# The mixer's output projection as seven products of halves, with memory's keys and values moved in front of it

## The chip, the cores and the metric

The kernel runs on one core of one Trainium2 chip. The metric is the device time of one execution in microseconds; the page of the profile and the trace come from one profiled execution. TensorE (PE) multiplies, VectorE (DVE) and ScalarE (ACT) work on tiles in on-chip memory, GpSimd (POOL) does a little elementwise work and issues the accumulating DMAs, SyncE (SP) issues most loads.

## The reference

One decoder layer for 512 tokens of width 2048 in float32: a mixer of three groups (12 heads of dilated attention, 8 heads of forgetting attention, 4 heads of gated linear attention, GLA) with one output projection, cross-attention of 4 heads into 256 memory tokens, and a gated MLP of width 5504; each has an RMSNorm in front and a residual add behind.

```python
mixed = jnp.concatenate([o_a, o_b, o_c], axis=-1)          # 512 x 2048
x = x + mixed @ w_out                                       # 2048 x 2048
mem_n = rms_norm(mem, mem_norm)
q = rms_norm(x, norm_cross) @ w_q
k, v = jnp.split(mem_n @ w_kv, 2, axis=-1)
...
x = x + memory_cross_attention(...)
x = x + conv_ffn(rms_norm(x, norm_ffn), w_up, conv_w, conv_b, w_down)
return rms_norm(x, norm_final)
```

## The kernel before

**Precision and form.** Activations lie transposed, 128 features on the partitions and 512 tokens along the row, in 16 tiles. Each operand of a large product is split into a high part (ScalarE's copy into float32r) and a low part (VectorE's subtraction); a product takes three matmuls: hi-hi, hi-lo, lo-hi (`mm3`, L367 to 373). Weights come as raw blocks of 128 x 1024 (512 KB), five buffers (`wraw`), and are split in halves of 512 columns into five buffers each of `whi` and `wlo` (`weights` L337 to 360, `split_weights` L326 to 332).

**Order.** Instructions are put in each engine's queue by a scheduler at build time, which goes by the order of the program and by what it reckons to be ready; each engine then works through its queue in that order. `issue_after(ins)` holds an instruction behind another one of the same engine. Work of the attention heads is written as generators; `tick` advances them by `rate` steps while the projections' units run (`run`, `W_A`, `W_B`, `W_O`, ...), so that the heads' small matmuls lie among the large ones. The score and transpose matmuls are put behind the last large one (`behind`).

**Mixer.** After the first projections and the GLA (`gla`, which ends with a power on POOL at L839), the pairs of heads of groups A and B are projected (`qk_units`) and attended (`attend`). Their 16 results, tiles of 128 x 512 in `self.mix`, lie in the pools `mc` and `mab` (`stream`, L266 to 269). The output projection then takes them as 16 pairs of split tiles (`mtile`, `split`, L314 to 319) and multiplies 16 x 16 blocks with 512 columns each: 32 weight blocks `w_o` of 512 KB, two for each of the 16 output tiles. The first halves of four output tiles run while the last heads finish (`W_O`). Each output tile is added to x from a raw load (`resid`, `raw_tile`) and squared for the next norm (`square`: even tiles are summed on POOL, odd ones on VectorE).

**Memory and cross-attention.** During the later output tiles, `memory` loads and splits the memory tokens and sums their squares. `cross` then runs memory's keys and values (8 blocks of `w_ck` with 256 columns, 8 blocks of `w_cv`) and, among them, the 16 splits of the residual for the queries (`more`) and the norm's root (`rms`, at unit `ST`). The query products, their heads and the output projection `w_co` follow.

**Sums of weights.** The MLP's up projection already works by seven products of halves: for blocks a11, a12, a21, a22 of the operand and b11 to b22 of the weights, seven products of sums of blocks take the place of eight (`product`, L1359 and following, `UP_ORDER`). Sums of weights for some tiles are made in DRAM by accumulating DMAs from POOL (`added`, L1258 to 1272, each behind the one before by `self.turn`): `first_sums` (11 transfers, held behind the last POOL square of the residual, `self.pooled`) and `up_sums` (8). They are issued at the beginning of the query products. During the cross output projection, `squares` (L1197 to 1204) makes ScalarE squares in three buffers `xsqt`, and POOL adds them by accumulating DMAs; `token_sums` (L1318 and following) makes the operands of the up projection.

## Time and profile before

| | us |
|---|---|
| median of 3 runs (lowest, highest) | 2306.24 (2304.97, 2306.7) |
| profiled execution | 2308.35 |
| its span, first to last instruction | 2306.2 |
| TensorE busy in the span | 2282.7 |
| VectorE, ScalarE, POOL busy | 1845.7, 1242.3, 204.9 |
| mean granted TensorE clock | 0.998 |

The span is what the trace covers; the profiled execution takes 2.15 us more. A matmul's record runs to its modelled end, which overlaps the next one's start, so the distance between starts is what a matmul costs. Rows of groups give the line, engine, operation, output and inputs by name, shapes, count, busy time and mean in ns. In a table of stretches the counts stand in brackets.

### The profile page before, as it was taken

What the parts mean: (1) busy time and instruction counts of PE and PEld (TensorE: products, weight loads), DVE (VectorE), ACT (ScalarE), POOL (GpSimd) and SP (SyncE); (2) the same over time, 40 slices, a digit from 0 to 9 for tenths busy, and PEclk for the clock granted to TensorE, in tenths of its full rate; (3) what the DMA queues carried; (4) which work ended last, traced back from release to release, by engine and by line L of the source; (5) the groups of instructions that cost most, each with busy time, mean ns of one, the idle gap of its engine ahead of it and who ended that gap; (6) DMA issues with size and microseconds to landing.
All of it is one profiled execution on the core that took longest, in us unless ns stands there. A gap on an engine that the chain in (4) does not pass through costs nothing.

```text
span 2306.2 us, 42646 instructions
## 1 busy us (share of the span) xinstructions
PE 2282.7 (99%) x15948; PEld 2140.1 (93%) x15948; DVE 1845.7 (80%) x3620; ACT 1242.3 (54%) x2545; POOL 204.9 (9%) x278
## 2 busy tenths in 40 slices
PE   9999999999999999999999999999999999999997
PEld 8798898888778888899999999999999999999997
DVE  7825666666797355699999999999999898999887
ACT  6323345655575254585555555555555575747454
POOL 3000000000002011121111111100000020101003
PEclk9999999999999999999999999999999999999999
DMA  6432122223224358587777778753334493736432
GB/s 217 152 97 83 49 98 91 93 87 96 87 80 153 110 180 218 132 233 180 214 209 213 205 209 215 199 184 122 130 126 140 142 337 103 277 115 230 154 122 84
DMA packets 130836, 355.47 MB, mean 154 GB/s; under 512 B 13653, under 2 KB 45333, under 8 KB 130181
## 3 DMA queue, kind: packets, MB, share of 16 engines
q1 hardware_dynamic: 87264, 268.28, 34.5%
q0 software_dynamic: 37168, 73.91, 14.6%
q10 hardware_dynamic: 6196, 10.57, 1.4%
q8 instruction: 125, 2.05, 0.4%
q14 instruction: 83, 0.67, 0.1%
HBM read 325.65 MB, written 76.07 MB: 174 GB/s over the span
## 4 chain that ended last, share of the span: by engine, by line
PE 91%; DVE 4%; DMA 2%; ACT 2%; issue 1%; POOL 0%; DVEq 0%; SPq 0%; ACTq 0%
PE acc L369 18%; PE acc L371 18%; PE acc L370 18%; PE psC L371 5%; PE psC L369 5%; PE psC L370 5%; PE psD L370 3%; PE psD L369 3%; PE psD L371 3%; PE acc L410 2%; PE acc L411 2%; PE acc L412 2%; PE psS L783 1%; PE psT L551 1%; PE psQ L371 1%; PE psQ L370 1%
## 5 line engine op out<-in xcount | busy, mean ns | idle before, releaser
L330 ACT ACTIVATE whi<-wraw 128x512 fp32r<-128x512 f32 (+2 forms) x814 | 466.1, 602 | 431.7 <-DVE wraw L1384 177.2
L331 DVE TENSOR_TENSOR wlo<-wraw,whi 128x512 fp32r<-128x512 f32 (+2 forms) x814 | 517.1, 655 | 83.5 <-ACT whi L330 78.8
L371 PE MATMUL acc<-sum,wlo 128*128 128x256 f32 x1956 | 549.3, 281 | 0.9 <-DVE wlo L331 0.8
L370 PE MATMUL acc<-sum,whi 128*128 128x256 f32 x1956 | 549.7, 281 | 0.0
L369 PE MATMUL acc<-sum,whi 128*128 128x256 f32 x1956 | 548.4, 280 | 0.0
L356 DVE TENSOR_TENSOR wlo<-wraw,whi 128x512 fp32r<-128x512 f32 (+2 forms) x336 | 223.0, 671 | 200.3 <-ACT whi L355 199.2
L355 ACT ACTIVATE whi<-wraw 128x512 fp32r<-128x512 f32 (+2 forms) x336 | 203.3, 610 | 325.1 <-PE acc L370 210.1
L371 PEld LDWEIGHTS acc<-sum,wlo 128*128 128x128 f32 x1956 | 368.5, 188 | 1.7 <-DVE wlo L331 1.7
L369 PEld LDWEIGHTS acc<-sum,whi 128*128 128x128 f32 x1956 | 368.5, 188 | 0.6 <-ACT whi L330 0.4
L370 PEld LDWEIGHTS acc<-sum,whi 128*128 128x128 f32 x1956 | 367.9, 188 | 0.0
L369 PE MATMUL acc<-xhi,whi 128*128 128x512 f32 (+1 forms) x848 | 334.8, 395 | 0.4 <-ACT fg L890 0.4
L371 PE MATMUL acc<-xhi,wlo 128*128 128x512 f32 (+1 forms) x848 | 329.1, 388 | 0.0
L370 PE MATMUL acc<-xlo,whi 128*128 128x512 f32 (+1 forms) x848 | 328.5, 388 | 0.0
L371 PE MATMUL psC<-sum,wlo 128*128 128x256 f32 x928 | 261.1, 281 | 0.0
L369 PE MATMUL psC<-sum,whi 128*128 128x256 f32 x928 | 260.3, 280 | 0.0
L370 PE MATMUL psC<-sum,whi 128*128 128x256 f32 x928 | 259.7, 280 | 0.0
L371 PEld LDWEIGHTS acc<-xhi,wlo 128*128 128x128 f32 x848 | 159.4, 188 | 32.0
L369 PEld LDWEIGHTS acc<-xhi,whi 128*128 128x128 f32 x848 | 159.6, 188 | 29.1 <-ACT fg L890 0.8
L370 PEld LDWEIGHTS acc<-xlo,whi 128*128 128x128 f32 x848 | 159.8, 188 | 28.5 <-DVE xlo L318 0.2
L369 PEld LDWEIGHTS psC<-sum,whi 128*128 128x128 f32 x928 | 175.0, 189 | 0.0
L370 PEld LDWEIGHTS psC<-sum,whi 128*128 128x128 f32 x928 | 174.7, 188 | 0.0
L371 PEld LDWEIGHTS psC<-sum,wlo 128*128 128x128 f32 x928 | 174.5, 188 | 0.0
(401 smaller groups left out, 4359.3 us busy)
## 6 DMA issues: line engine op xcount, KB each, us to landing
wraw<-in_w_up SPq DMA_DIRECT2D x127, 512.0 KB, 6.2
b<-in_w_up SPq DMA_DIRECT2D x42, 512.0 KB, 4.5
wraw<-in_w_o SPq DMA_DIRECT2D x32, 512.0 KB, 3.5
wraw<-in_w_d SPq DMA_DIRECT2D x34, 448.0 KB, 4.4
wraw<-in_w_d SPq DMA_DIRECT2D x36, 384.0 KB, 4.6
wraw<-in_w_qka SPq DMA_DIRECT2D x24, 512.0 KB, 3.5
gd<-sq SPq DMA_DIRECT2D x40, 256.0 KB, 6.2
wraw<-two SPq DMA_DIRECT2D x20, 512.0 KB, 5.5
```

What stands on the lines that cost most here:

```text
L330: nc.scalar.activation(hi, r, AF.Copy)
L331: nc.vector.tensor_tensor(lo, r, hi.bitcast(F32), op=ALU.subtract)
L355: nc.scalar.activation(hi, r, AF.Copy)
L356: nc.vector.tensor_tensor(lo, r, hi.bitcast(F32), op=ALU.subtract)
L369: nc.tensor.matmul(out, lh, rh, start=start, stop=False, skip_group_check=more)
L370: nc.tensor.matmul(out, lh, rl, start=False, stop=False, skip_group_check=more)
L371: last = nc.tensor.matmul(out, ll, rh, start=False, stop=stop, skip_group_check=more)
L410: self.nc.tensor.matmul(o, xh[:, tt], wh, start=(k == 0), stop=False)
L411: self.nc.tensor.matmul(o, xh[:, tt], wl, start=False, stop=False)
L412: self.last = self.nc.tensor.matmul(o, xl[:, tt], wh, start=False, stop=(k == KT - 1))
L551: nc.tensor.transpose(tp[:, b * P:(b + 1) * P], pt[:, b * P:(b + 1) * P], self.ident)
L783: nc.tensor.matmul(sc[:, c * 64:(c + 1) * 64], kk[:, c * P:(c + 1) * P], qe[:, c * 64:(c + 1) * 64], start=True, stop=True)
```

## The change

- The 16 mixed tiles now lie in eight pairs (`mixed`, `stream`), in an order (`MIX_PAIRED`) that puts the blocks for the halves side by side.
- `out_sums`, right behind the GLA, issues for each of eight units the four sums of weight blocks in DRAM: eight transfers of 512 KB by `added`, 64 in all, on POOL. The first waits for the GLA's power, which is now `self.turn`; what was held behind the old `turn` is held behind `forgot`.
- `keys_values` takes the place of `memory` and of the first part of `cross`. It runs right behind the last B projection, with the last heads among its units (`W_M`): memory is loaded, split and squared in freed activation slots (`xlo`, `xhi`); keys and values are kept as float32 (`mkey`, `mval`) and split later (`halved`, in the first query product).
- `project` makes the seven operands of each of four groups (`operands`, the function that the up projection uses too) and runs eight units of seven products, 24 matmuls of 256 columns each, for two output tiles of 128 x 512 at a time. x is loaded into the tiles of the residual, and each product's result is added or subtracted there. In the last unit the products have another order (`OUT_ORDER`), and the splits for the queries are made there, in tiles that the products leave (`more`).
- In `cross` the norm's root and `halved` stand behind the first unit of the first query head.

```diff
+OUT_ORDER = (4, 5, 1, 6, 7, 3, 2)
...
+MIX_PAIRED = [MIX_ORDER[4 * v + 2 * e + i] for v in range(4) for i in range(2) for e in range(2)]
...
-        nc.gpsimd.tensor_tensor(ssf, ssf, self.mhalf, op=ALU.pow)
+        self.turn = nc.gpsimd.tensor_tensor(ssf, ssf, self.mhalf, op=ALU.pow)
...
-            self.turn = nc.scalar.activation(self.fg[:, t, :], ps[:, 384:G0], AF.Copy, scale=self.rs[:, t:t + 1])
+            self.forgot = nc.scalar.activation(self.fg[:, t, :], ps[:, 384:G0], AF.Copy, scale=self.rs[:, t:t + 1])
...
         es_core.close()
         es_gl.close()
+        self.out_sums()
...
-        units = [self.out_units(d["w_o"], n, Lazy(), evac_o(n)) for n in range(KT)]
-        self.rate = W_O / 2
-        for n in range(4):
-            units[n][0]()
-            self.tick()
-        self.rate = 0
+        self.keys_values()
         self.flush()
         es_ab.close()
         es_vv.close()
...
-        for n in range(4):
-            units[n][1]()
-        mem = self.memory()
-        for n in range(4, KT):
-            for u in units[n]:
-                u()
-                if n >= M0:
-                    next(mem, None)
+        self.project()
+
+    def keys_values(self):
+        nc, d = self.nc, self.d
+        raws = [self.xtile("xlo") for _ in range(8)]
+        mem = []
+        for j, raw in enumerate(raws):
+            two = raw.rearrange("p (i c) -> p i c", c=MEM)
+            nc.sync.dma_start(out=two, in_=d["memT"][j // 2][:, j % 2 * 2:j % 2 * 2 + 2, :])
+            for i in range(2):
+                t = self.xtile("xhi", F32R)
+                mem.append(self.split_to(t[:, :MEM], t[:, MEM:], two[:, i, :], self.gain(4, 2 * j + i)))
+            nc.scalar.activation(raw, raw, AF.Square)
+            if j > 1:
+                nc.vector.tensor_tensor(raws[j % 2], raws[j % 2], raw, op=ALU.add)
...
+        units = self.nat_units(d["w_cv"], 0, lambda k: mem[k], MT, evac_v)
+        units.insert(6, stats)
+        units += [u for h in range(X_HEADS) for u in self.out_units(d["w_ck"], h, mem, evac_k(h), MEM)]
+        self.run(units, W_M)
+
+    def out_sums(self):
+        self.o_pre = []
+        for n in range(KT // 2):
+            b11, b12, b22, b21 = [self.d["w_o"][4 * n + i] for i in range(4)]
+            t = [self.dr.tile([P, 1024], F32, name="o%d%d" % (n, i)) for i in range(4)]
+            self.added(t, b11, b12, b22, b21)
+            self.o_pre.append(t)
+
+    def operands(self, v, y, s, place):
...
+        src = {1: a11, 2: a12, 4: a22, 5: sa, 6: sb, 3: sb, 7: sa}
+        made = {5: (a22, a21, ALU.subtract), 6: (sa, a11, ALU.add), 3: (sb, a12, ALU.subtract),
+                7: (a21, a11, ALU.subtract)}
+        def part(j):
+            if j in made:
+                nc.vector.tensor_tensor(src[j], made[j][0], made[j][1], op=made[j][2])
+            th, tl = [place[j, v, n].rearrange("p (i c) -> p i c", c=HT) for n in range(2)]
+            split = nc.scalar.activation(th, src[j], AF.Copy)
...
+            nc.vector.tensor_tensor(tl, src[j], th.bitcast(F32), op=ALU.subtract)
+        return part
+
+    def project(self):
...
+        pa, pb = self.pool(self.es_a, "oa", "right"), self.pool(es_b, "ob", "right")
...
+        for v in range(NV - 1):
+            for j in (1, 5, 2, 6, 3):
+                parts[v](j)
...
+        def unit(n):
+            x = self.stream(n)
+            nc.sync.dma_start(out=x, in_=d["xT"][n])
+            w = [d["w_o"][4 * n + i] for i in range(4)]
+            pre = self.o_pre[n]
+            src = {1: w[0], 5: pre[0], 2: w[3], 6: pre[1], 3: w[2], 4: pre[2], 7: pre[3]}
...
+            for j in OUT_ORDER if last else UP_ORDER:
+                if n == 0:
+                    for v in range(NV) if j in (4, 7) else (NV - 1,):
+                        parts[v](j)
+                ps = bank[j][:, :HT]
+                self.product(j, self.halves(self.up_raw(src[j])), ps, j in (1, 5, 6, 4), True)
+                after(j, ps)
+                if last and j == 5:
+                    more(8, 4, 5)
+                if last and j == 7:
+                    more(6, 7, 1)
+            self.x1 += [x[:, 0, :], x[:, 1, :]]
+            for dt in (2 * n, 2 * n + 1):
+                self.square(dt, self.x1[dt], sqs, lambda c: tmps[dt % 2])
+            if last:
+                more(2, 7, 1)
...
+        def halved():
+            for a, th, tl in [(self.mkey[h], kh[h], kl[h]) for h in range(X_HEADS)] + list(zip(self.mval, vh, vl)):
+                nc.scalar.activation(th, a, AF.Copy)
+                nc.vector.tensor_tensor(tl, a, th.bitcast(F32), op=ALU.subtract)
+
+        def root():
+            box["R"] = self.rms(self.sqs, S, self.con.tile([P, S], F32, name="R", tag="R"))
...
         for h in range(X_HEADS - 1):
-            self.run(self.out_units(d["w_cq"], h, hs, evac_q(h, 0, NT)), W_X)
+            units = self.out_units(d["w_cq"], h, hs, evac_q(h, 0, NT))
+            if h == 0:
+                units.insert(1, root)
+                units.insert(2, halved)
+            self.run(units, W_X)
```

In `after(j, ps)`, two results are copied by ScalarE (`s1`, `s5`), and nine additions or subtractions of 128 x 256 on VectorE put the seven products together in the tiles of x.

More of the change, by code (lines that the diff above doesn't have):

```diff
@@ L72 @@
 W_B = 4
-W_O = 6
+W_M = 3
 W_X = 8
 WARM = 8
-M0 = 8
-H0 = 4
-H1 = 6
-ST = 4
 E0 = 14
@@ L264, in pool, with stream, mixed @@
         return es.enter_context(self.tc.tile_pool(name=name, bufs=1, side=side, reuse_waits="tile"))
-    def stream(self, k):
-        pool = self.mc if k < 6 else self.mab
-        return pool.tile([P, S], F32, name="str", tag="str", bufs=6 if k < 6 else 10)
+    def stream(self, n):
+        pool = self.mc if n < 3 else self.mab
+        return pool.tile([P, 2, S], F32, name="str", tag="str", bufs=3 if n < 3 else 5)
+    def mixed(self, m):
+        n = MIX_ORDER.index(m)
+        if n // 2 not in self.pairs:
+            self.pairs[n // 2] = self.stream(n // 2)
+        self.mix[m] = self.pairs[n // 2][:, n % 2, :]
+        return self.mix[m]
     def advance(self, n):
@@ L309, in xslot, with xtile @@
     def xslot(self, n=S):
-        hi = self.xp.tile([P, n], F32R, name="xhi", tag="xhi", bufs=KT, padded_shape=[P, S])
-        lo = self.xp.tile([P, n], F32R, name="xlo", tag="xlo", bufs=KT, padded_shape=[P, S])
-        return hi, lo
+        return self.xtile("xhi", F32R, n), self.xtile("xlo", F32R, n)
+    def xtile(self, tag, dtype=F32, n=S):
+        return self.xp.tile([P, n], dtype, name=tag, tag=tag, bufs=KT, padded_shape=[P, S])
     def split(self, src, n=S):
@@ L1327, in token_sums @@
             y.append(t)
[L1328 to L1344 removed]
+        sums = [tmp.tile([P, 2, HT], F32, name=n, tag=n, bufs=1) for n in ("sa", "sb")]
+        return self.operands(v, y, sums, place)
     def up_raw(self, u, pool=None):
```

199 lines of the change are left out of this document (94 added, 105 removed).

## The prediction

> **What bounds the kernel now.** I read the page's first lines, then a table by stretches (length, then busy time of PE, PEld, DVE, ACT and POOL with instruction counts, granted clock, DMA share, GB/s), then the order of the instructions where it matters.
>
> ```profile
> span 2306.2 us, 42646 instructions
> PE 2282.7 (99%) x15948; PEld 2140.1 (93%) x15948; DVE 1845.7 (80%) x3620; ACT 1242.3 (54%) x2545; POOL 204.9 (9%) x278
> ```
>
> ```profile
> 600.00:649.00 49.00, 47.49 (x236) 39.28 (x235) 36.53 (x100) 30.28 (x68) 0.00 (x0) 1.00 0.27 89
> 649.00:661.50 12.50, 12.50 (x62) 10.41 (x61) 12.49 (x38) 12.28 (x30) 0.00 (x0) 1.00 0.17 50
> 661.50:706.50 45.00, 43.81 (x219) 34.93 (x218) 39.17 (x115) 28.49 (x69) 0.00 (x0) 1.00 0.26 92
> 706.50:853.00 146.50, 146.50 (x656) 121.55 (x656) 72.63 (x113) 60.77 (x113) 23.49 (x24) 1.00 0.43 142
> 853.00:898.00 45.00, 45.00 (x288) 41.07 (x287) 31.53 (x53) 26.83 (x45) 4.10 (x4) 1.00 0.95 248
> 898.00:966.00 68.00, 67.69 (x377) 56.12 (x376) 40.27 (x99) 30.52 (x78) 8.20 (x10) 1.00 0.66 157
> 966.00:1015.00 49.00, 48.95 (x258) 42.11 (x257) 46.82 (x77) 45.89 (x84) 11.30 (x14) 1.00 0.71 170
> 1400.00:1700.00 300.00, 300.00 (x2546) 300.00 (x2545) 279.87 (x439) 160.68 (x287) 16.47 (x21) 1.00 0.56 168
> ```
>
> TensorE has work almost everywhere at full clock, so the kernel is as long as its matmuls plus the places where something else comes late. 661.5 is the end of the last B projection. From there to 706.5 the last attention heads run among the first matmuls of the output projection and VectorE is near its limit (39.17 of 45). From 706.5 to 853 TensorE alone binds; then memory's keys and values, 45 us. In 966 to 1015 (cross output projection, operands of the up projection) ScalarE (45.89 of 49) and VectorE (46.82) bind.
>
> **The matmuls.** What counts is the distance of their starts. The start time and duration of two hi-hi matmuls of the output projection, 13 groups of three apart, then the first copy of each up tile:
>
> ```profile
> 708.62 0.40 PE L369 MATMUL acc<-xhi,whi 128*128 128x512 f32 x1
> ...
> 717.48 0.39 PE L369 MATMUL acc<-xhi,whi 128*128 128x512 f32 x1
> ```
>
> ```profile
> L1414 ACT ACTIVATE s<-acc x42: 363/384/385, 1029.4 to 1843.3; 128x256 f32<-128x256 f32 x42
> ```
>
> 8.86 us by 39 is 0.227 us for 512 columns. An up tile is seven products of 24 matmuls of 256 columns: (1843.3 - 1029.4) / 41 = 19.85 us, 0.118 each. The projection has 16 x 16 x 3 = 768 of the wide ones, 174.5 us. After the change it is eight such units, 1344 narrow ones, 158.8 us. **Saved: 15.7 us.**
>
> The Trainium skill ("TensorE: Matmul & The Clock Gate", section "Back-to-back issue gap") gives 131 ns for 512 columns and 81 ns for 128; by a straight line between, 256 would cost 0.75 of 512, not half. The trace does not agree: 227 and 118 ns, 0.52.
>
> **What VectorE gets before and in the first unit.** Counts in 661.5 to 706.5, and three operand subtractions in a row on the chain (start, duration):
>
> ```profile
> L356 DVE TENSOR_TENSOR wlo<-wraw,whi 128x512 fp32r<-128x512 f32 x10 | 6.8, 687 | 0.7 <-PE psS L539 0.5
> L318 DVE TENSOR_TENSOR xlo<-str,xhi 128x512 fp32r<-128x512 f32 x7 | 4.7, 680 | 0.7 <-ACT xhi L317 0.7
> ```
>
> ```profile
> L318 DVE TENSOR_TENSOR xlo<-str,xhi x16: 669/680/693, 650.0 to 706.4; 128x512 fp32r<-128x512 f32 x16
> ```
>
> ```profile
> L371 PE MATMUL acc<-xhi,wlo 128*128 128x512 f32 x43 | 17.0, 395 | 0.0
> ```
>
> ```profile
> 975.24 1.81 DVE sum L1342 x3
> ```
>
> ```profile
> L574 DVE TENSOR_TENSOR str<-psO,ot x20: 682/689/695, 388.2 to 705.0; 64x512 f32<-64x512 f32 x20
> ```
>
> ```profile
> L323 DVE SCALAR_TENSOR_TENSOR xlo<-str,gains,xhi 128x512 fp32r<-128x512 f32 x6 | 4.4, 742 | 0.0
> L1063 DVE TENSOR_TENSOR kf<-acc,R 128x256 f32<-128x256 f32 x4 | 1.7, 420 | 0.3
> ```
>
> So 0.60 us for each 128x512 in a row (0.68 alone), 0.66 with a gain (0.74 alone), and about 0.35 for 128x256 (0.42 alone); the last two are estimates, less the same 0.07. From 661.5 to the last product of unit 0 VectorE then has:
> - the heads: 39.17 less 17 x 0.60 = 28.9;
> - keys and values: 32 weight splits (19.4), 16 memory splits of 256 columns (5.6), 6 square sums (3.6), less the 6.6 that it can do in the place of nine activation splits and two more before 661.5: 22.0; four key results 1.4;
> - operands of the seven products, all four groups: 28 low parts and 16 sums or differences, 44 x 0.60 = 26.6. The 16 low parts that they replace fell into 650 to 706. They cannot start earlier: their tiles lie where the attention's and values' tiles lie until the last head's result at 705 (L574), or in activation slots in use until 661;
> - unit 0: 14 weight splits 8.5, six results 2.1.
>
> Sum 89.5. TensorE has there: 45 less 129 projection matmuls (3 x 43) x 0.227 = 15.7 for the heads with their gaps; keys and values with the memory statistics 46; unit 0 19.85: 81.5. VectorE is 8 over at full use, 13 at the 95% that it reaches in 966 to 1015. **Added: 11 us**, bounds 5 and 17. Units 1 to 6 give VectorE 14 splits, 9 results and a square sum, 12.3 of 19.85, and hide all of it. ScalarE is nowhere over: it gains some 7 us of operand parts.
>
> **The last unit and what follows.** The first query matmul, behind the last of memory's values:
>
> ```profile
> 897.68 0.39 PE L412 MATMUL acc<-whi,mlo 128*128 128x512 f32 x1
> 897.91 0.39 PE L369 MATMUL acc<-xhi,whi 128*128 128x512 f32 x1
> ```
>
> The 16 splits of the residual for these queries lay beside memory's products (853 to 898, VectorE 31.5 of 45). Now they lie in the last unit: 12.3 + 16 x 0.66 = 22.9 on VectorE against 19.85, and behind it come the two norm splits, three norm steps and eight splits of keys and values, 7 us, in the first query product. That is some 3 us more than fits; the later splits have some time. **Added: 2.5 us**, bounds 0 and 6. So the query products would start 15.7 - 11 - 2.5 = **2 us earlier** than at 897.91.
>
> **The weight sums.** 64 transfers, eight for each unit, on POOL's queue, behind the GLA's power at 318:
>
> ```profile
> 318.04 2.91 POOL L839 TENSOR_TENSOR oss<-oss,mhalf 128x16 f32<-128x16 f32 x1 [31.62 <-DVE oss L838]
> 843.50 1.35 POOL L1046 TENSOR_TENSOR sq<-sq,sqt 128x512 f32<-128x512 f32 x1 [20.97 <-ACT sqt L1044]
> 844.79 2.10 POOL L1308 DMA_DIRECT2D pre<-in_w_up  x4
> 849.69 1.09 POOL L1312 DMA_DIRECT2D pre<-in_w_up  x1 [2.81 <-DMA pre<-in_w_up]
> ...
> 908.54 0.90 POOL L1262 DMA_DIRECT2D up<-in_w_up  x1
> ...
> 948.49 1.01 POOL L1262 DMA_DIRECT2D up<-in_w_up  x1 [6.60 <-DMA up<-in_w_up]
> 971.32 0.90 POOL L1204 DMA_DIRECT2D sq<-xsqt  x1 [21.81 <-ACT xsqt L1203]
> ```
>
> ```profile
> up<-in_w_up POOLq DMA_DIRECT2D x12, 512.0 KB, 7.4
> up<-up POOLq DMA_DIRECT2D x4, 512.0 KB, 3.9
> ```
>
> One set of eight takes 40 us from first issue to last (908.54 to 948.49), so some 42 with the next issue. With the lighter traffic before 660 (DMA share 0.27 against 0.66), 42 to 48: done at 321 + 8 x 44 = 673, bounds 657 and 705. Unit 0 starts near 725: hidden. The sums' traffic falls beside the attention's weight loads; 1400 to 1700 carries loads and such sums at DMA 0.56 with TensorE full: nothing, bounds 0 and 5. A unit then loads seven blocks of 512 KB in 19.85 us, 185 GB/s, about what that stretch moved (168): nothing. Its x load waits on SP until a pair of mixed tiles is free (in unit 0: until an operand 4 or 7 of the first group), with weight loads queued behind; five weight buffers, 14 us of products, cover it: nothing, bounds 0 and 3. POOL's power for memory's statistics stands behind the 64 sums; it is wanted near 695 (661.5, 21.8 for 96 value matmuls at 0.227 and 12 of the heads' 15.7): nothing either, but that is the thinnest cover here.
>
> **The next sums on that queue** are the up projection's, and they carry the price. They wait for the residual's last POOL square. It ended at 844.8, 53 us ahead of the query products, under memory's products; now it ends some 3 us behind their start. From that square to the issue of the last sum went 948.5 - 844.8 = 103.7 us. Part of it was traffic (853 to 898 at DMA 0.95). Without: copies 4.9, seven sums at about 6 us (40), the set of eight 40: 85; bounds 80 and 103.7. POOL is then free at 88 us behind the start of the query products, but the first square of the cross residual wants it at 971.3 - 897.9 = 73.4. It comes 15 us late.
>
> ```profile
> L1203 ACT ACTIVATE xsqt<-str x14: 614/618/633, 970.4 to 1011.3; 128x512 f32<-128x512 f32 x14
> L1204 POOL DMA_DIRECT2D sq<-xsqt x14: 862/864/899, 971.3 to 1015.0; - x14
> ...
> DMA to landing us min/median/max: 3.3/5.4/7.9
> ```
>
> ```profile
> 981.38 0.62 ACT L1203 ACTIVATE xsqt<-str 128x512 f32<-128x512 f32 x1
> ```
>
> The squares have three buffers. The fourth, at 981.38, needs the first one's transfer, 971.3 + 5.4: slack 4.7. So ScalarE would stand some 10 us in its queue, in the stretch where it is busy 45.89 of 49, with the weight splits of the cross output and the up operands behind the waiting square, then VectorE, then TensorE behind those. **Added: 10 us**, bounds 0 (in time) and 25 (103.7 + 3 - 73.4 - 4.7 = 29, less what an earlier start takes off). I take 10 as the 0.66 stretch is nearest to the new traffic.
>
> The Trainium skill ("TensorE: Matmul & The Clock Gate", section on the 16 sub-arrays) calls the GpSimd queue strict first in, first out; the POOL rows above, sums before squares, agree. Its page "DMA: Bandwidth & Descriptors", section "Anatomy of one DMA — SWDGE (gpsimd) path", puts such a transfer at 2.0 us plus bytes / 436e3, 3.2 us for 512 KB. The trace has 3.9 for a copy and 7.4 for a sum; by the page the first rival below would hold.
>
> **Sum.** -15.7 + 11 + 2.5 + 10 = **+8 us**. The profiled execution took 2308.35 us, 2.15 around its span; the runs' median is 2306.24, so I put the change on the median: **2314 us**, its own range 2308 to 2330.
>
> **Rivals.**
> 1. *The sums are out of the way.* If the 19 transfers take copies' time, 19 x 3.9 = 74, or the squares are issued between them, no square waits: -15.7 + 11 + 2.5 = -2, **2304** (2299 to 2309). For it: 21.81 us of spare time before. Against it: 7.4 for a sum.
> 2. *Faster: VectorE does not bind either.* It sat idle 12 us in 600 to 649; if parts of the operands and the first splits fall there, or are spread into unit 1, only the matmuls count: -15.7 + 2.5 = **2293** (2288 to 2299). Against it: the tiles' places.
> 3. *Slower: POOL's 64 sums run late.* At 50 us a set they end at 721, 20 to 25 us behind the wish of memory's statistics; ScalarE's copy of memory's values waits, and with it every later weight split: 2314 + 20 = **2334**. It decides from 47 us a set.
> 4. *The narrow matmul at 0.75 of the wide one* in this kernel's new place: 1344 x 0.170 = 228.9, +54: **2360**. Against it: the up units have them at 0.118. The first page's straight line would give this.
>
> **Chances.** Forecast 0.37, first rival 0.28, second 0.24, third 0.08, fourth 0.03. Within 0.2% is 2301.6 to 2310.9, about what a measurement can tell. Faster: all of the second and 0.08 of the first, 0.32. Same: 0.18 of the first and 0.05 of the forecast, 0.23. Slower 0.45. The range 2291 to 2330 leaves out the lower edge of the second, most of the third and the fourth.
>
> **What would show it.** Right: unit 0 near 30 us with TensorE waiting for VectorE's operand parts, units 1 to 6 at 19.85; POOL's first square issue of the cross residual well behind its ScalarE square, and ScalarE idle for that transfer. Wrong: units slower than 19.85; ScalarE waiting for a POOL power near 700; the query products more than 8 us from 896; the squares issued as soon as they are made.

## The result, and the profile after

| | median, us | runs | profiled span, us | clock |
|---|---|---|---|---|
| before | 2305.60 | 4 (2304.47 to 2306.70) | 2306.2 | 0.998 |
| after | 2339.64 | 4 (2338.79 to 2340.83) | 2337.0 | 0.991 |

The changed kernel takes 1.0148 times as long, 95% interval 1.013 to 1.0166: 34 us slower. The direction was as forecast, the size was not (+8). The first lines of the page of after:

```profile
span 2337.0 us, 44230 instructions
PE 2280.4 (98%) x16532; PEld 2161.0 (92%) x16532; DVE 1912.7 (82%) x3751; ACT 1280.1 (55%) x2617; POOL 248.7 (11%) x333
```

TensorE is busy 2.3 us less than before, although the narrow matmuls should have taken 15.7 off it, and it is idle some 33 us more. To find the place I compared two marks that both kernels have: the first scaled query (`cqf`, behind the first query product), and the first copy of an up tile. The rows are from the view of one tile; they give minimum, median and maximum duration in ns, then the first and the last start. First before, then after:

```profile
L1157 DVE SCALAR_TENSOR_TENSOR cqf<-acc,R x5: 423/690/692, 909.0 to 957.9; 128x512 f32<-128x512 f32 x3, 128x256 f32<-128x256 f32 x2
```

```profile
L1231 DVE SCALAR_TENSOR_TENSOR cqf<-acc,R x5: 425/692/693, 923.0 to 972.0; 128x512 f32<-128x512 f32 x3, 128x256 f32<-128x256 f32 x2
L1478 ACT ACTIVATE s<-acc x42: 361/386/389, 1061.2 to 1873.9; 128x256 f32<-128x256 f32 x42
```

The first query is 14.0 us late (909.0 to 923.0). From there to the first up tile it takes 138.2 us against 120.4 (1029.4 in the prediction less 909.0): 17.8 us more. Behind that the two run alike within 1.2 us. Up to the last B projection, near 661, both kernels run alike. So there are two losses, 31.8 us together. (The two profiled executions, 2308.35 and 2338.79, lie 30.4 us apart, the medians 34.0.)

**The first loss, 661 to 772.** The table by stretches of after (columns as in the prediction):

```profile
660.00:665.00 5.00, 4.37 (x21) 3.14 (x19) 5.00 (x16) 5.00 (x15) 0.00 (x0) 1.00 0.69 172
665.00:670.00 5.00, 1.86 (x8) 0.90 (x7) 5.00 (x15) 5.00 (x14) 0.00 (x0) 0.89 0.00 0
670.00:675.00 5.00, 0.00 (x0) 0.00 (x0) 4.77 (x16) 4.15 (x9) 0.00 (x0) 0.50 0.21 48
675.00:680.00 5.00, 4.35 (x15) 3.49 (x15) 4.76 (x9) 1.45 (x4) 0.00 (x0) 0.59 0.50 125
...
735.00:770.00 35.00, 29.88 (x224) 27.36 (x223) 32.59 (x58) 19.60 (x36) 0.00 (x0) 1.00 0.69 224
770.00:890.00 120.00, 120.00 (x1010) 119.89 (x1009) 88.80 (x149) 64.82 (x112) 10.30 (x8) 1.00 0.64 194
890.00:895.00 5.00, 2.75 (x17) 2.14 (x17) 5.00 (x9) 3.81 (x8) 0.00 (x0) 0.91 0.00 0
```

Where TensorE stands, VectorE is full: 660 to 680 (19.53 of 20, and ScalarE 10.00 of 10 in the first half) and 735 to 770. Between them it has gaps:

```profile
661.50:722.00 60.50, 51.27 (x287) 42.22 (x288) 52.62 (x149) 42.73 (x102) 0.82 (x1) 0.92 0.41 122
722.00:772.00 50.00, 44.88 (x349) 42.25 (x348) 47.50 (x85) 33.56 (x62) 0.27 (x1) 1.00 0.63 201
```

The waits of 655 to 690 (engine, tile and line that waited, what ended it: us in total, times, longest):

```profile
PE acc L420 <- DVE wlo L365: 7.3, 1, 7.3
...
ACT xhi L331 <- DMA xlo<-in_memT: 3.7, 1, 3.7
```

The memory loads are issued from 649.0 on, as the last B projection's matmuls leave the slots that they go to, and the first has landed at 655.4; all 16 memory splits and 8 squares then lie on ScalarE and VectorE, among the heads' own work, ahead of the value weights' splits, and TensorE waits 7.3 us for one of these. That delays the heads too. The last head's result and the first low part of an operand, in order of time (start, duration), and the first residual tile done, on POOL:

```profile
722.25 0.69 DVE L583 TENSOR_TENSOR str<-psO,ot 64x512 f32<-64x512 f32 x1
722.98 1.29 DVE L1026 TENSOR_TENSOR osum<-str,osum 128x512 fp32r<-128x512 f32 x2
```

```profile
771.73 2.54 POOL L1132 TENSOR_TENSOR sq<-str 128x512 f32<-128x512 f32 x2 [69.08 <-DVE str L1059]
786.10 1.29 POOL L1138 TENSOR_TENSOR sq<-sq,xlo 128x512 f32<-128x512 f32 x1 [11.82 <-ACT xlo L1136]
806.07 1.30 POOL L1138 TENSOR_TENSOR sq<-sq,xlo 128x512 f32<-128x512 f32 x1 [18.68 <-ACT xlo L1136]
...
886.20 1.30 POOL L1138 TENSOR_TENSOR sq<-sq,xlo 128x512 f32<-128x512 f32 x1 [18.92 <-ACT xlo L1136]
911.46 2.26 POOL L1138 TENSOR_TENSOR sq<-sq,xlo 128x512 f32<-128x512 f32 x1 [23.97 <-ACT xlo L1136]
913.67 2.04 POOL L1387 DMA_DIRECT2D pre<-in_w_up  x4
...
1006.34 1.01 POOL L1341 DMA_DIRECT2D up<-in_w_up  x1 [9.28 <-DMA up<-in_w_up]
1006.99 2.19 POOL L1283 DMA_DIRECT2D sq<-xsqt  x2
```

The operands start at 723 (the prediction took 705) and unit 0 is done at 771.7. From unit 1 to unit 6 the units come at 19.97 to 20.2 us (806.07 - 786.10 is the first), near the forecast's 19.85; the last takes 25.3 (911.46 - 886.20).

Unit 1 is done only 14.4 us behind unit 0. While unit 0's last product (`acc<-xhi`) waits for its parts, TensorE puts matmuls of unit 1's first products (`acc<-osum`, `psC<-xlo`) between:

```profile
769.09 0.28 PE L378 MATMUL acc<-osum,whi 128*128 128x256 f32 x1
769.45 0.38 PE L379 MATMUL acc<-xhi,whi 128*128 128x256 f32 x1
```

Some 50 of unit 1's 168 are done when unit 0 ends, 6 us of work at 0.119 each. So unit 0's mark overstates what was lost, and unit 1's is the safer one.

**The second loss, 1006 to 1030.** The same rows show POOL's queue: the up projection's sums from 913.67 to 1006.34, and only then the residual's squares. The waits of 980 to 1030:

```profile
ACT xsqt L1282 <- DMA sq<-xsqt: 18.7, 1, 18.7
DVE wlo L365 <- ACT whi L364: 18.3, 1, 18.3
...
PE acc L378 <- ACT sum L1023: 16.1, 1, 16.1
```

ScalarE waits 18.7 us for a buffer of squares, VectorE for the weight split behind it, TensorE for the operand behind that.

### The profile page after: what moved, and what is told of

Read it like the earlier page. It is cut to its first block, busy times and chain, and to the rows that moved or that the text cites. A ratio compares the mean times of both kernels' runs of the same rounds, so it can differ in the third digit from the quotient of the medians.

```text
span 2337.0 us, 44230 instructions
## 1 busy us (share of the span) xinstructions
PE 2280.4 (98%) x16532; PEld 2161.0 (92%) x16532; DVE 1912.7 (82%) x3751; ACT 1280.1 (55%) x2617; POOL 248.7 (11%) x333
## 3 DMA queue, kind: packets, MB, share of 16 engines
q0 software_dynamic: 55088, 107.47, 21.6%
## 4 chain that ended last, share of the span: by engine, by line
PE 55%; issue 2%; DVE 2%; DMA 2%; ACT 1%; POOL 1%; DVEq 0%; ACTq 0%; POOLq 0%
PE acc L380 10%; PE acc L379 10%; PE acc L378 10%; PE psC L380 5%; PE psC L378 5%; PE psC L379 5%; PE psD L379 3%; PE psD L380 3%; PE psD L378 3%; PE psQ L380 1%; PE psQ L379 1%; PE psQ L378 1%; DMA up<-in_w_up 1%; DMA pre<-in_w_up 1%; DVE sum L1026 0%
## 5 line engine op out<-in xcount | busy, mean ns | idle before, releaser
L339 ACT ACTIVATE whi<-wraw 128x512 fp32r<-128x512 f32 (+2 forms) x926 | 536.0, 606 | 500.2 <-DVE wraw L1448 176.5
L340 DVE TENSOR_TENSOR wlo<-wraw,whi 128x512 fp32r<-128x512 f32 (+2 forms) x926 | 596.2, 663 | 108.5 <-ACT whi L339 101.1
L365 DVE TENSOR_TENSOR wlo<-wraw,whi 128x512 fp32r<-128x512 f32 (+2 forms) x272 | 179.5, 668 | 155.3 <-ACT whi L364 154.9
L364 ACT ACTIVATE whi<-wraw 128x512 fp32r<-128x512 f32 (+2 forms) x272 | 162.4, 605 | 235.5 <-PE acc L379 123.8
L378 PE MATMUL acc<-xhi,whi 128*128 128x512 f32 (+1 forms) x720 | 271.0, 376 | 1.2 <-ACT whi L364 0.6
L380 PE MATMUL acc<-xhi,wlo 128*128 128x512 f32 (+1 forms) x720 | 265.7, 369 | 0.0
L379 PE MATMUL acc<-xlo,whi 128*128 128x512 f32 (+1 forms) x552 | 214.5, 389 | 0.0
L379 PEld LDWEIGHTS psC<-sum,whi 128*128 128x128 f32 x928 | 174.5, 188 | 0.0
L380 PEld LDWEIGHTS acc<-xhi,wlo 128*128 128x128 f32 x720 | 135.7, 188 | 22.9 <-DVE wlo L365 0.4
L378 PEld LDWEIGHTS acc<-xhi,whi 128*128 128x128 f32 x720 | 135.9, 189 | 21.2 <-ACT whi L364 0.9
L420 PE MATMUL acc<-wlo,xhi 128*128 128x384 f32 (+2 forms) x352 | 125.9, 358 | 8.2 <-DVE wlo L365 8.2
```

What stands on the lines that cost most here:

```text
L339: nc.scalar.activation(hi, r, AF.Copy)
L340: nc.vector.tensor_tensor(lo, r, hi.bitcast(F32), op=ALU.subtract)
L364: nc.scalar.activation(hi, r, AF.Copy)
L365: nc.vector.tensor_tensor(lo, r, hi.bitcast(F32), op=ALU.subtract)
L378: nc.tensor.matmul(out, lh, rh, start=start, stop=False, skip_group_check=more)
L379: nc.tensor.matmul(out, lh, rl, start=False, stop=False, skip_group_check=more)
```

## The experiments

All are edits of the changed kernel. Ratios are against the kernel before, run on the same chip; the changed kernel itself has 1.0148. "Unit 0 done" is POOL's first square of the residual, "query" and "up" are the two marks. The marks are of one execution each: e1_sums changes nothing ahead of 771, and its last head is 1.5 us earlier than that of after, so differences of 1 or 2 us between marks show nothing. The intervals of e2_lazy, e4_spread, e5_memsq, e6_low, e9_leavesq and e10_heads overlap that of after; what their medians suggest is not shown by them alone.

| run | what | ratio, 95% interval | median, us | last head | unit 0 done | query | up |
|---|---|---|---|---|---|---|---|
| after | | 1.0148, 1.013 to 1.0166 | 2339.6 | 722.3 | 771.7 | 923.0 | 1061.2 |
| e1_sums | sums early | 1.0055, 1.004 to 1.007 | 2318.0 | 720.8 | 771.9 | 920.8 | 1039.9 |
| e2_lazy | memory splits by units | 1.0131, 1.0116 to 1.0146 | 2335.4 | 717.2 | 769.6 | 919.6 | 1058.3 |
| e3_leave | 16 low parts left out | 1.0100, 1.0085 to 1.0115 | 2329.1 | 719.4 | 755.7 | 910.2 | 1050.9 |
| e4_spread | query splits spread | 1.0147, 1.013 to 1.0164 | 2338.0 | 720.3 | 771.8 | 921.4 | 1057.4 |
| e5_memsq | squares to POOL | 1.0160, 1.0145 to 1.0175 | 2343.2 | 722.9 | 773.1 | 926.0 | 1059.5 |
| e6_low | 10 low parts to POOL | 1.0167, 1.0152 to 1.0182 | 2344.2 | 719.9 | 775.2 | 925.0 | 1064.4 |
| e7_all | e1, e2, e4, e5, e6 | 1.0083, 1.0066 to 1.0100 | 2322.9 | 722.6 | 777.1 | 924.8 | 1044.0 |
| e8_best | e1, e2, e4 | 1.0038, 1.0023 to 1.0053 | 2314.4 | 719.3 | 771.6 | 919.6 | 1038.9 |
| e9_leavesq | 6 squares left out | 1.0124, 1.0107 to 1.0141 | 2335.6 | 718.2 | 767.6 | 921.7 | 1060.3 |
| e10_heads | heads ahead | 1.0124, 1.0108 to 1.0139 | 2333.1 | 704.6 | 763.9 | 915.5 | 1055.4 |
| e11_sums_heads | e1, e4, e10 | 1.0024, 1.0014 to 1.0033 | 2310.2 | 705.6 | 764.9 | 912.9 | 1032.0 |
| e12_more | e11, e2, more rate | 1.0016, 1.0007 to 1.0025 | 2309.3 | 706.3 | 763.4 | 911.7 | 1030.8 |
| e13_bare | e11, e3, e9 | 0.9974, 0.9964 to 0.9984 | 2299.1 | 702.4 | 747.7 | 901.4 | 1020.6 |

### POOL's queue: e1_sums

```diff
-            nc.gpsimd.tensor_tensor(sqs[dt], x, x, op=ALU.mult)
+            self.held = nc.gpsimd.tensor_tensor(sqs[dt], x, x, op=ALU.mult)
...
-        with self.tc.issue_after(self.pooled.ins):
+        with self.tc.issue_after(self.held.ins):
...
-                self.square(dt, self.x1[dt], sqs, lambda c: tmps[dt % 2])
+                self.square(dt, self.x1[dt], sqs, lambda c: tmps[dt % 2], nc.vector)
```

(`square` takes the engine of its sum as a new last argument.)

> The 19 transfers of the up projection's sums are held behind POOL's square of the first residual tile (771.7 us in the changed kernel) in place of its last one (911.5), and the residual's square sums behind the output projection are all made on VectorE, so that no square stands between them: they should then run from 772 to some 860, beside units 1 to 5. Theory (the POOL queue is the price of the cross output projection, 17.7 us from 971.8 to 1029.4 as the before had it): ScalarE's wait of 18.7 us for the third buffer of squares goes below 2, the first copy of an up tile comes at 1043 to 1045, and the time is 2340 - 17.7 = 2322 us, 2319 to 2325. Rival (ScalarE and VectorE are full there anyway, 45.9 and 46.8 of 49 us before, and the queue only hides it): the wait turns into others, first up copy at 1055 or later, 2335 to 2340. Second rival (the sums' traffic, with seven weight blocks a unit, is too much for the DMA): the wait goes, but units 1 to 5 take over 20.3 us each, 2325 to 2335.

2318.0 us, 21.6 below the changed kernel. From query to up it takes 119.1 us, before 120.4: the second loss is gone whole. POOL in e1_sums, the first transfer, the last, and the first square:

```profile
774.42 2.04 POOL L1387 DMA_DIRECT2D pre<-in_w_up  x4
...
895.28 1.01 POOL L1341 DMA_DIRECT2D up<-in_w_up  x1 [9.02 <-DMA up<-in_w_up]
983.12 0.89 POOL L1283 DMA_DIRECT2D sq<-xsqt  x1 [86.82 <-ACT xsqt L1282]
```

Now POOL waits for ScalarE. The sums take 121 us there, longer than the 93 of after, and it costs nothing:

```profile
770.00:890.00 120.00, 119.94 (x1007) 119.62 (x1006) 87.98 (x155) 64.22 (x112) 16.89 (x20) 1.00 0.93 267
```

DMA share 0.93 in place of 0.64, with TensorE full. The theory holds, with a gain 1 us over its range (2319 to 2325); both rivals fall. The run makes two edits at once, the earlier hold and the square sums off POOL's queue, and does not part them.

### VectorE ahead of unit 0: e2_lazy, e3_leave, e4_spread

e2_lazy: loads as before, the splits made when a value unit asks for them.

```diff
-        for j, raw in enumerate(raws):
...
-                mem.append(self.split_to(t[:, :MEM], t[:, MEM:], two[:, i, :], self.gain(4, 2 * j + i)))
+        def made(k):
+            while len(mem) < (4, 6, 8, 10, 12, 16, 16, 16)[k // 2]:
...
-        units = self.nat_units(d["w_cv"], 0, lambda k: mem[k], MT, evac_v)
+        units = self.nat_units(d["w_cv"], 0, made, MT, evac_v)
```

> Memory's splits and squares are no longer issued in one block ahead of the keys and values, but two or three loads' worth with each of the first six value units, behind that unit's weight splits; loads, work and sums stay the same. Theory (TensorE lost 9 to 11 us in 660 to 680, waiting for weight splits that stood behind the block of 16 memory splits and 8 squares, and by the lower clock behind it): TensorE has over 18 of 20 us in 660 to 680, all behind it comes 9 us earlier, 2340 - 9 = 2331 us, 2328 to 2333. Rival (it is VectorE's total up to the end of unit 0 that binds, as the prediction summed it): the values start earlier, but TensorE waits as much longer for the operands in unit 0, the first unit's end stays near 771.7, 2337 to 2341.

```profile
660.00:680.00 20.00, 17.47 (x82) 13.28 (x82) 19.12 (x54) 19.43 (x47) 0.00 (x0) 1.00 0.42 115
680.00:700.00 20.00, 16.00 (x74) 12.21 (x73) 18.81 (x56) 10.72 (x26) 0.71 (x1) 0.83 0.34 90
```

This is e2_lazy. TensorE gets 17.47 of the first 20 us, where after had 10.59, but 16.00 of the next 20, where after had 19.61. VectorE is near full in both. 4.2 us are won by the medians, 2.2 at unit 0; the intervals of the two ratios overlap. Most of the wait was moved, as the rival said.

e3_leave:

```diff
-            nc.vector.tensor_tensor(tl, src[j], th.bitcast(F32), op=ALU.subtract)
+            if not skip or j not in (5, 6, 3, 7):
+                nc.vector.tensor_tensor(tl, src[j], th.bitcast(F32), op=ALU.subtract)
```

> Leaves out the low parts of the output projection's operands 5, 6, 3 and 7 (16 subtractions on VectorE, 0.60 us each, 9.6 us); the products read low parts of other operands in their place, in the same number of matmuls. Theory (VectorE is full from 661 to the end of unit 0, and TensorE lost some 8 us in 735 to 770 to it): the loss goes, 2340 - 8 = 2332 us, 2330 to 2334, with TensorE at over 18 of 20 us in 740 to 760. Rival (the losses in unit 0 are those of the x load, of the weights' transfers or of the clock behind the earlier stall): 2337 to 2341.

```profile
755.65 2.54 POOL L1134 TENSOR_TENSOR sq<-str 128x512 f32<-128x512 f32 x2 [55.82 <-DVE str L1061]
775.50 1.29 POOL L1140 TENSOR_TENSOR sq<-sq,xlo 128x512 f32<-128x512 f32 x1 [17.30 <-ACT xlo L1138]
```

Unit 0 is done 16.1 us earlier, but here TensorE finishes unit 0 before it begins unit 1 (19.85 us between the marks in place of 14.4). At unit 1's mark it is 10.6 us (786.10 to 775.50), by the medians of the whole kernel 10.6 as well, for 9.6 us of VectorE's work. So VectorE binds there, about one for one.

e4_spread:

```diff
-                if last and j == 5:
-                    more(8, 4, 5)
-                if last and j == 7:
-                    more(6, 7, 1)
+                if last and j in (5, 1, 6):
+                    more(2 if j == 6 else 3, 4, 5)
+                if last and j in (7, 3):
+                    more(3, 7, 1)
```

> The 14 splits for the queries in the last unit of the output projection are no longer issued as a block of eight behind product 5 and one of six behind product 7, but three, three and two behind products 5, 1 and 6, and three and three behind 7 and 3, so that the weight splits of the next product stand behind three of them at most. Theory (the last unit took 25.3 us against 20 because its weight splits stood behind the block): it takes 21 to 22, 2340 - 4 = 2336 us, 2335 to 2337. Rival (VectorE has 22.9 us of work there and 7 more in the first query product, in whatever order): the unit is shorter but the first query product is later by as much, 2339 to 2341.

1.0147 against 1.0148: no difference. The last unit takes 23.3 us in place of 25.3, where the theory had 21 to 22. From unit 0's end to the query it is 149.6 us; e1_sums, with the old order, has 148.9. So no effect of the order is shown.

### More room for VectorE on POOL: e5_memsq, e6_low, e7_all

e5_memsq:

```diff
-            nc.scalar.activation(raw, raw, AF.Square)
+            nc.gpsimd.tensor_tensor(raw, raw, raw, op=ALU.mult)
             if j > 1:
-                nc.vector.tensor_tensor(raws[j % 2], raws[j % 2], raw, op=ALU.add)
+                nc.gpsimd.tensor_tensor(raws[j % 2], raws[j % 2], raw, op=ALU.add)
```

> Memory's eight squares go from ScalarE to POOL, and their six sums from VectorE to POOL, which has nothing to do from 656 to 700 us; all else as in the changed kernel. Theory (in 660 to 670 VectorE and ScalarE are both full, 10.0 of 10, and TensorE waits for weight splits behind that work): 8 x 0.61 = 4.9 us come off ScalarE and 6 x 0.60 = 3.6 off VectorE, TensorE stands 3 to 5 us less in 660 to 680, 2340 - 4 = 2336 us, 2334 to 2337. Rival (the order alone does it: the block of memory splits still stands ahead of the value weights' splits): 2338 to 2340. Second rival (the gain is lost again in unit 0, whose operands come when they came): PE busy in 660 to 680 rises by 3 or more, but POOL's square of the first residual tile stays at 771 to 772, 2338 to 2340.

e6_low:

```diff
-            nc.vector.tensor_tensor(tl, src[j], th.bitcast(F32), op=ALU.subtract)
+            eng = nc.gpsimd if low and (j == 4 or j in (1, 2) and v < 3) else nc.vector
+            eng.tensor_tensor(tl, src[j], th.bitcast(F32), op=ALU.subtract)
```

> Ten low parts of the output projection's operands (1 and 2 of the first three groups, 4 of all four) go from VectorE to POOL, at 1.3 us or more each there. Theory (VectorE's work up to the end of unit 0 binds one for one: 9.6 us left out gave 10.6 us): 10 x 0.60 = 6 us off VectorE, 2340 - 6 = 2334 us, 2332 to 2336, and POOL's square of the first residual tile at 765 to 767. Rival (POOL is slower than 1.35 us beside a busy VectorE, or slows VectorE, so that TensorE waits for POOL's parts): 2338 or more, with waits of TensorE for osum parts of POOL.

Both missed: nothing won, and unit 0 is 1.4 and 3.5 us later (e6_low's is beyond the spread of the marks). VectorE in e6_low, while POOL makes six low parts (720.46 to 730.30):

```profile
719.13 0.69 DVE L365 TENSOR_TENSOR wlo<-wraw,whi 128x512 fp32r<-128x512 f32 x1 [1.10 <-ACT whi L364]
...
723.93 1.78 DVE L365 TENSOR_TENSOR wlo<-wraw,whi 128x512 fp32r<-128x512 f32 x1
725.64 1.78 DVE L1021 TENSOR_TENSOR sq<-sq,str 128x512 f32<-128x512 f32 x1
727.34 1.79 DVE L365 TENSOR_TENSOR wlo<-wraw,whi 128x512 fp32r<-128x512 f32 x1
729.05 1.79 DVE L1027 TENSOR_TENSOR osum<-sq,osum 128x512 fp32r<-128x512 f32 x1
730.77 0.68 DVE L365 TENSOR_TENSOR wlo<-wraw,whi 128x512 fp32r<-128x512 f32 x1
```

```profile
L1027 POOL TENSOR_TENSOR osum<-str,osum x6: 1293/1742/1755, 720.5 to 728.5; 128x512 fp32r<-128x512 f32 x6
```

A subtraction of 0.69 us takes 1.78 beside POOL, one of POOL's 1.74 in place of 1.29: they take turns. In e5_memsq it is the memory splits (mean of one from 655 to 780, first after, then e5_memsq):

```profile
L332 DVE SCALAR_TENSOR_TENSOR xhi<-xlo,gains,xhi 128x256 fp32r<-128x256 f32 x16 | 7.1, 478 | 3.7 <-ACT xhi L331 3.7
```

```profile
L332 DVE SCALAR_TENSOR_TENSOR xhi<-xlo,gains,xhi 128x256 fp32r<-128x256 f32 x14 | 11.9, 878 | 0.0
```

> All of it together: the up projection's sums early and the residual's square sums on VectorE (2318.0 us alone, 21.6 less than the changed kernel), memory's splits by units (4.2 less alone), the query splits spread (1.7 less), memory's squares on POOL, ten low parts on POOL. If VectorE's work binds one for one and each step counts: 2318 - 4 - 1.5 - 3 - 6 = 2303 us, 2299 to 2306, the same as the kernel before or a little faster. Rival (memory's splits by units and memory's squares on POOL cure the same wait, and what binds after that is the order of unit 0's operands, which start at 705 when the last head leaves its tiles): 2307 to 2312.

2322.9: no better than e1_sums alone (2318.0; the intervals just touch), and far from the sum. What the two POOL edits cost at least eats up what the order won.

### e8_best and e9_leavesq

e8_best is e1_sums, e2_lazy and e4_spread without the POOL edits.

> The up projection's sums early and the residual's square sums on VectorE (2318.0 us alone), with memory's splits by units (4.2 less alone) and the query splits spread (1.7 less alone), and nothing else on POOL. Theory (the POOL instructions beside VectorE's are what made the run with all of it 2322.9: the same steps without them come to their sum): 2318 - 4 - 1.5 = 2312 us, 2309 to 2315. Rival (memory's splits by units only move the wait within the heads' stretch, and the spread splits gain nothing behind an early sum): 2317 to 2320.

2314.4, as the theory had it; against e1_sums the intervals overlap. It is 8.5 us below e7_all, with intervals apart, so POOL's 24 instructions did cost that much.

e9_leavesq leaves out the squares and sums that e5_memsq moved, but for the first two squares:

```diff
-            nc.scalar.activation(raw, raw, AF.Square)
-            if j > 1:
-                nc.vector.tensor_tensor(raws[j % 2], raws[j % 2], raw, op=ALU.add)
+            if j < 2:
+                nc.scalar.activation(raw, raw, AF.Square)
```

> Leaves out six of memory's eight squares (ScalarE, 6 x 0.61 = 3.7 us) and their six sums (VectorE, 6 x 0.60 = 3.6 us), so that keys and values are scaled by a wrong norm; order and all else as in the changed kernel. The run that moved this work to POOL gained nothing. Theory (it was POOL's work beside VectorE's that took it back: memory's low parts on VectorE went from 0.48 to 0.88 us each there): without any of it 660 to 680 loses 4 to 6 us less, 2340 - 4 = 2336 us, 2333 to 2337. Rival (what TensorE waits for there is the order, the 16 splits of memory ahead of the value weights, and VectorE's total counts only in unit 0): 2338 to 2341.

2335.6, 4 us, inside the theory's range; but its four times lie between 2330.7 and 2339.7, so theory and rival are not told apart. Unit 0 is done 4.2 us earlier (e5_memsq: 1.4 later). The profiled execution took 2339.7, and in it the gain is lost again by the query.

### The heads ahead: e10_heads to e13_bare

```diff
-W_VB = 3
+W_VB = 5
...
-W_B = 4
+W_B = 6
```

> The heads' work is moved ahead by its rate alone: 5 and 6 steps in place of 3 and 4 beside the units of the last value and B projections, so that some 30 of the heads' 85 VectorE instructions behind the last B projection lie before 655, where VectorE has 12 of 20 us of work. Theory (VectorE's total from 655 to the end of unit 0 binds): some 10 us of VectorE's and 5 of TensorE's work leave that stretch, the last head leaves its tiles 8 us earlier, and with the operands of unit 0 earlier too the query products start 5 to 9 us earlier: 2340 - 7 = 2333 us, 2330 to 2336. Rival (the stretch before 655 gets the wait in place of it, as the heads' chain of engines is as long there): the last B projection ends 4 us or more behind 660.7, and 2337 to 2342.

2333.1, as expected. Nothing is taken out; heads' work moves to before 655, where VectorE had room. The last head is done at 704.6 in place of 722.3, unit 0 7.8 us earlier, the query 7.5. The next run, against e1_sums, shows the gain clear of noise.

> The up projection's sums early with the residual's square sums on VectorE, the query splits spread, and the heads' work moved ahead by its rate. If the three add up (21.6, 1.7 and the 7 that the rate should bring): 2340 - 21.6 - 1.5 - 7 = 2310 us, 2306 to 2314, still not below the kernel before. If the rate brings nothing: 2316 to 2319.

2310.2: the sum, and below e1_sums (2318.0) with intervals apart, where the spread query splits alone showed no gain. Still 1.0024 of before.

> As the run with the sums early, the query splits spread and the heads ahead (2310.2 us), with the heads' rate raised further (6 and 8 steps) and memory's splits by units. Theory (what is left ahead of the query products is VectorE's order in 660 to 690 and its total up to unit 0): both help some, 2310 - 3 = 2307 us, 2304 to 2310, level with the kernel before. Rival (the rate is used up: the last heads need the last B projection's results, 48 of their instructions stand behind it against 56; and the split order only moves the wait): 2309 to 2313.

2309.3 (rates 6 and 8), with unit 0 at 763.4 (e11: 764.9). That lies in both ranges, and the interval overlaps that of e11: no gain is shown, as the rival had it; why the higher rate brings none is not. No version with all of the work came below the kernel before.

> As the run with the sums early, the query splits spread and the heads ahead (2310.2 us), and it leaves out the low parts of operands 5, 6, 3 and 7 (16 x 0.60 us of VectorE) and six of memory's squares with their sums (3.6 us each of VectorE and ScalarE); the results are wrong by that, the matmuls are all there. Theory (all that the change loses ahead of the query products is VectorE's work, so the 15.7 us of the matmuls are there once it is out of the way): units 1 to 6 at 19.97 us, the first scaled query at 909 - 11 to 909 - 5 = 898 to 904, and 2310 - 10 = 2300 us, 2296 to 2303, below the kernel before. Rival (part of the saving never was there: narrow matmuls cost more outside the plain units, or loads bind): the first scaled query at 908 or later, 2305 to 2310.

2299.1, 0.9974 of before, and the query at 901.4. (Six squares of ScalarE are left out as well, 3.7 us.) Its table by stretches where after lost most:

```profile
660.00:680.00 20.00, 19.04 (x88) 14.05 (x87) 18.62 (x54) 17.65 (x41) 0.00 (x0) 1.00 0.47 141
...
735.00:770.00 35.00, 35.00 (x297) 35.00 (x297) 26.26 (x46) 17.74 (x31) 5.62 (x7) 1.00 0.99 342
```

TensorE is full in 735 to 770, 297 matmuls in place of 224. The saving of the matmuls is in the kernel; VectorE's work hides it.

## Why the prediction was right or wrong

**Matmuls, -15.7: right.** The units come at 19.97 us (forecast 19.85), so eight of them save 14.7 of 174.5. With 13.2 us of VectorE's work out of the way (e13_bare) the query came 7.6 us ahead of before. By the prediction's own terms: 15.7 less 2.5 for the last unit, less the 4.7 that unit 0 is still behind 743 (747.7; 661.5 + 81.5 of TensorE's work) makes 8.5.

**VectorE up to the end of unit 0, +11 (5 to 17): this is the step that failed. VectorE does bind there, but the cost was about 23 us, twice the term and over its upper bound.** By the prediction unit 0 would end at 661.5 + 81.5 + 11 = 754 and unit 1 at 773.9. They ended at 771.7 and 786.1. Unit 0's mark would make the term 28.7, but some 6 us of unit 1 were done by then; by unit 1's mark it is 11 + 12.3 = 23. The query came at 923.0 where the prediction had 907 (754 + 7 x 19.85 + 2.5 + 11.1, the last being 909.0 - 897.91). Of these 16 us, 12 lie ahead of unit 1's end, 1 in units 2 to 6, and 3 in the last unit. What went wrong in the step:
- It added VectorE's work to one total, 89.5 us, as if any piece could fill any gap. VectorE did 100.1 us there (52.62 + 47.50) and was idle 10.4, 7.9 of it ahead of 722, mostly between its two jams: memory's block at 660 to 680, and the operands from 723 on.
- It put the operands' start at 705, the last head's result *before*. But the heads run among the keys and values, and the first jam delays them to 722.3. Moving them back to 704.6 by the rate alone (e10_heads) gave 7.8 us at unit 0; that run also takes heads' work out of the stretch, so it does not part the two.
- It took memory's splits for spread work. They came as a block behind a load that arrived at 655.4, and TensorE did 43 matmuls in 660 to 680, where it had done 100 in the 20 us before: some 57 x 0.2 = 11.4 us. In 735 to 770 it did 224, where e13_bare did 297: 73 x 0.118 = 8.6 us. That is 20 of the 23; the rest is not told apart. The block is not the whole of the first jam: taken apart (e2_lazy) it moved the wait more than it cured it.
- Of the 10.6 us by which VectorE's work was larger, 5.4 (9 x 0.60) is nine weight splits of unit 1 made ahead (23 of the units' kind by 772 where the step counted 14), which go with the matmuls of unit 1 done ahead. Where the other 5.2 come from is open:

```profile
L340 DVE TENSOR_TENSOR wlo<-wraw,whi 128x512 fp32r<-128x512 f32 x23 | 16.1, 722 | 1.4 <-ACT whi L339 1.4
```

**Last unit, +2.5 (0 to 6): the mechanism right, within its bounds, but twice the size.** It took 25.3 us, 5.4 over 19.85. That from unit 0's mark to the query it is 151.3 us, against a forecast of 152.6, is luck: unit 1 is short by what was done ahead, and the last unit long. TensorE stands there (busy 2.75 of 5 in 890 to 895): it waits 1.9 us for a weight split, and its matmuls then start 0.21 us apart until 897.4 in place of 0.118. No effect of the order of the splits is shown (e4_spread).

**POOL's queue, +10 (0 to 25): the mechanism right to the instruction, the size 17.8.** The wanted time was right: the first square came 62.3 us behind the query before (971.3 - 909.0), and 984.5 + 0.6, 62.1 behind it, after. The start of the sums was right: 9.3 us ahead of the query, forecast 8.1. What was short is the length of the 19 transfers: 85 us forecast, 93.3 measured (913.67 to 1006.99), so POOL came 22 us late in place of 15, and ScalarE waited 18.7. The upper bound of that term, 103.7, held it. The first rival (the sums are out of the way) was false as the kernel stands, and is what e1_sums makes true. An estimate from the Trainium skill ("DMA: Bandwidth & Descriptors", section "Anatomy of one DMA — SWDGE (gpsimd) path"), 3.2 us for 512 KB by its formula, would have had the 19 done in 61 us; the trace does not agree.

**out_sums, nothing: right.** The last of the 64 was issued at 655.25 and, with the median of 7.3 us from issue to landing (last row), done near 662, inside the 657 to 705 given. The memory loads of 649 to 655 landed in 4.7 to 6.3 us beside them; no run tests whether they would have come sooner without (DMA share 0.83 in 640 to 660, before 0.19). Memory's power waited for VectorE, not for the sums, so the third rival is false:

```profile
655.25 1.05 POOL L1341 DMA_DIRECT2D o<-in_w_o  x1 [8.35 <-DMA o<-in_w_o]
701.83 0.82 POOL L449 TENSOR_TENSOR rsm<-rsm,mhalf 128x2 f32<-128x2 f32 x1 [45.53 <-DVE rsm L448]
```

```profile
o<-in_w_o POOLq DMA_DIRECT2D x48, 512.0 KB, 7.3
```

**x loads, nothing (0 to 3): right**; VectorE waited 1.0 us for one. **The second rival** (VectorE does not bind) is false by e3_leave. **The fourth** (narrow matmuls at 0.75) is false by the units' 19.97.

**The sum as measured.** At the query: -15.7 + 1 (units 2 to 6) + 23.3 + 5.4 = 14.0 us late; with 17.8 for POOL's queue and 1.0 won back behind it, 30.8, the difference of the two spans.

The range ended at 2330, although the upper ends of all terms together (17, 6 and 25) give 2306.2 + 32.3 = 2339: it took them as if only one could come at its upper end. Here one came over its bound (23 of 17) and two far up in theirs (17.8 of 25, 5.4 of 6).

## What to carry to other kernels

A sum of an engine's work over a stretch is a bound from below only: cut it where a load arrives or a tile comes free, and check each piece, and check whether the marks taken from the old trace (here the last head's result) move with the change. When a stage gets shorter or later, list what is held behind its last instruction on a queue and who is next on it; moving the hold to an earlier instruction, with the square sums off that queue, gave 21.6 of the 34 us here. Before a loss is read off one mark, look whether the engine had begun the next piece by then. Take work off a full VectorE to another time, not to POOL.

## What the runs showed of the hardware

**VectorE and POOL take turns.** 0.69 us became 1.78 on VectorE and 1.29 became 1.74 on POOL in e6_low, for float32 instructions of 128 x 512 with two inputs in SBUF. The Trainium skill ("SBUF — State Buffer", section "SBUF: two separate sides") says that a VectorE instruction with two SBUF inputs and a GpSimd one that reads SBUF lock each other out for the whole instruction; the trace agrees. In e5_memsq a tensor_scalar with one tile as input did not go free either (128 x 128: 1.28 us, 0.28 in after, beside a POOL sum that starts at 660.49 and takes 1.32):

```profile
660.62 1.28 DVE L553 TENSOR_SCALAR pt<-pt,sm 128x128 f32<-128x128 f32 x1
```

**A stop of TensorE costs more than its length.** In after TensorE does nothing from 668.4 to 675.65, and then runs slower for a while:

```profile
675.65 0.80 PE L420 MATMUL acc<-wlo,xhi 128*128 128x512 f32 x1 [7.27 <-DVE wlo L365]
...
677.10 0.63 PE L420 MATMUL acc<-wlo,xhi 128*128 128x512 f32 x1
677.52 0.63 PE L421 MATMUL acc<-whi,xhi 128*128 128x512 f32 x1
...
679.18 0.39 PE L420 MATMUL acc<-wlo,xhi 128*128 128x512 f32 x1
679.41 0.39 PE L421 MATMUL acc<-whi,xhi 128*128 128x512 f32 x1
```

The starts lie 0.42 us apart for 3.2 us, then 0.23, with a granted clock of 0.50 in 670 to 675 and 0.59 in 675 to 680: some 1.5 us lost on top of the stop. The Trainium skill ("TensorE: Matmul & The Clock Gate", section "What's actually happening") has half clock until about 3.4 us of work have gone by; the trace agrees.

**Sums in DRAM stretch without harm.** The same 19 transfers took 93 us in after and 121 in e1_sums, with the DMA engines at 0.93 in 770 to 890, and TensorE was busy for 119.94 of those 120 us. What they cost in after was the place in POOL's queue, not the traffic.
